# Twenty-two unread products on TensorE at the end of a two-layer diffusion trunk

## Chip, cores and metric

One core of a Trainium2 chip runs the whole kernel as one program. The metric is the device time of one execution in microseconds; lower is better.

## The reference

One inference step of a trunk with two layers, on 128 prompt tokens and 512 sample tokens with 1024 features each. Layer 0 is a Conformer convolution branch, layer 1 a bidirectional Mamba-2 (SSD) branch. The change touches the very end, the output projection of layer 1 and the RMSNorm after it:

```python
y = rms_norm(y.reshape(b, l, SSD_GROUPS, SSD_INNER // SSD_GROUPS), ...)
out = y @ w_out                       # 2048 -> 1024
yp = yp + gt_p * out_p                # gated residual, prompt
ys = ys + gt_s * out_s                # gated residual, sample
y_prompt = rms_norm(yp, final_norm_g) # x * rsqrt(mean(x*x) + 1e-6) * g
y_sample = rms_norm(ys, final_norm_g)
```

## The kernel before, in words

The activations lie transposed in on-chip memory: 8 tiles `x[0..7]` of 128 features by 640 tokens. The tokens are worked on in two halves of 320 (`HN`); half b holds columns `b * 320` to `b * 320 + 319`, 64 of the prompt and 256 of the sample. Every dense product is made in three terms from operands that are split into a high and a low part (`wh`, `wl` for weights, `yh`, `yl` for activations, type fp32r), 320 columns wide at the end of the program.

Layer 1 is written as many small generators (chains). A planner (`Order`) starts with estimated durations, picks the next operation over all chains by its estimated time and priority, and emits it; so the order of each engine's queue is fixed when the program is built. Each engine then works through its own queue strictly as it stands, and waits on counters of the other engines.

The end of the program, in the order that matters here:

- `last_products(b)`, first for half 1, then for half 0: for each of the 8 output tiles 4 steps of 3 products (line 1342, `o` in the rows), that is 12 products of 320 columns.
- `last_residual(b, m, ...)`: when tile m is done, VectorE adds it with its gate to `x[m]` (line 1311, two instructions), ScalarE squares it (line 1316, `sq`), GpSimd adds most squares into one accumulator (line 1321). The last tiles are scaled by the norm's weight on ScalarE at once (line 1325).
- `final(b)`: TensorE sums the squares over the features with a matmul against a column of ones (`column_sums`, line 177, one column each). It does so in two parts: the first two accumulators, then the last tile's square, `PARTS` of the tokens at a time. VectorE copies the first part (line 1357) and adds the second (line 1363) into `sm`; ScalarE takes the root (line 1364, `rc`); VectorE the reciprocal (line 1365); TensorE spreads it over all partitions (`spread`, line 182); VectorE multiplies the first tiles of `x` by it (line 1370); ScalarE copies it (line 1378, `rb`) and GpSimd multiplies the rest (line 1381); each finished tile is stored (line 1385, `o_y`), 160 KB at a time, 16 stores in all. `sm` and `rc` have one buffer each, which both halves use in turn.

In the program as built, the second part of half 1's sums, the first part of half 0's and the second part of half 0's stand on TensorE behind all the products, and both spreads stand behind these. An instruction of `column_sums` or `spread` on fp32 data shows as two matmul records in the trace, so 6, 12 and 6 sums and 6 and 6 spreads.

Of the kernel before, what the change touches and what calls it, by code (L numbers as in the profile page):

```python
# [7 lines left out]
F32 = mybir.dt.float32  # L8
# [5 lines left out]
P = 128  # L14
NT = 640
NP = 128
HN = 320
# [24 lines left out]
def trunk(ctx: ExitStack, tc: tile.TileContext, a: dict):  # L42
# [5 lines left out]
    V, S, G, T = nc.vector, nc.scalar, nc.gpsimd, nc.tensor  # L48
# [6 lines left out]
    def c(name, i=0, n=1):  # L55
        o = _C[name][0] + i
        if o >= NCST:
            return cst0[0][:, o - NCST : o - NCST + n]
        return cst[:, o : o + n]
# [36 lines left out]
    def gain(l, m, cd):  # L96
        return mod[l][:, 8 + m // 2, m % 2, cd : cd + 1]
# [75 lines left out]
    def column_sums(ps, tiles, parts=FIVE):  # L173

        for i, (t0, nt) in enumerate(parts):
            for n, t in enumerate(tiles):
                last = T.matmul(ps[0:nt, i : i + 1], lhsT=t[:, t0 : t0 + nt], rhs=ones[:, 0:1], start=n == 0, stop=n == len(tiles) - 1)
        return last

    def spread(ps, col, parts=FIVE):  # L180
        for i, (t0, nt) in enumerate(parts):
            last = T.matmul(ps[:, t0 : t0 + nt], lhsT=col[0:nt, i : i + 1].broadcast_to([nt, P]), rhs=eye[0:nt, 0:nt], start=True, stop=True)
        return ps[:, 0 : parts[-1][0] + parts[-1][1]], last
# [55 lines left out]
    def mm(name):  # L239
        return pp.tile([P, 2, 512], F32, tag="mm", bufs=2, name=name)  # L240
# [51 lines left out]
    with tc.tile_pool(name="l0", bufs=1) as lp:  # L292
# [33 lines left out]
        for i in range(3):  # L326
            t = lp.tile([P, 2, 30], F32, name=f"eb{i}")
# [191 lines left out]
        yh, yl, scaled = [], [], []  # L519
# [97 lines left out]
    if True:  # L617
# [8 lines left out]
        for i in range(2):  # L626
            t = lp.tile([P, 646], F32, name=f"up{i}")
# [19 lines left out]
        def tr(name):  # L647
            return lp.tile([P, NT], F32, tag="yhl", bufs=8, name=name)[:, 0:384]
# [4 lines left out]
        xr, rp, e, q, t, u, v, one = (tr(n) for n in ("xr", "rp", "e", "q", "t", "u", "v", "one"))  # L653
# [8 lines left out]
        PE, ACT, VE, PO, SP, VL = range(6)  # L662

        class Order:
# [12 lines left out]
            def post(self, key, t):  # L677
                assert key not in self.keys, key
                self.keys[key] = t

            def put(self, name, t):
                self.rings[name].append(t)

            def start(self, gen, ready=0.0, name=None):
                self.count += 1
                ch = [gen, ready, PRIO.get(name or gen.__name__, 1), self.count, None, None]
                self.chains.append(ch)
                self.advance(ch, None)
# [70 lines left out]
        post, put, start = run.post, run.put, run.start  # L759

        def op(eng, dur, fn, table=None):
            return "op", ((eng, dur, fn, table),)
# [4 lines left out]
        def key(*ks):  # L767
            return ("key",) + ks

        def get(name):  # L770
            return "get", name
# [8 lines left out]
        def vec(n):  # L780
            return 0.12 + 0.001 * n
# [107 lines left out]
        grp = [{} for _ in range(NG)]  # L889
# [387 lines left out]
        w3 = {}  # L1277
# [25 lines left out]
        accs = {0: [], 1: []}  # L1303
# [3 lines left out]
        def last_residual(b, m, ps, ring):  # L1307
            tok = slice(b * HN, b * HN + HN)
            for cd, sl in SEGS:
                xv = x[m][:, tok][:, sl]  # L1310
                t = yield op(VE, vec(sl.stop - sl.start) + 0.08, lambda: V.scalar_tensor_tensor(out=xv, in0=ps[:, sl], scalar=gain(1, m, cd), in1=xv, op0=ALU.mult, op1=ALU.add))
            put(ring, t)
            nm, bufs = SQ[b]
            yield get(nm)
            sq = lp.tile([P, 512], F32, tag=nm, bufs=bufs, name="sq")[:, 0:HN] if b == 0 else lp.tile([P, HN], F32, tag=nm, bufs=bufs, name="sq")
            t = yield op(ACT, 0.47, lambda: S.activation(out=sq, in_=x[m][:, tok], func=AF.Square))
            if m == 0 or m > KD - 3:
                accs[b].append(sq)
            else:
                yield key(("acc", b, m - 1))  # L1320
                t = yield op(PO, 0.85, lambda: G.tensor_add(out=accs[b][0], in0=accs[b][0], in1=sq))
                put(nm, t)
            post(("acc", b, m), t)
            if m >= KD - REST[b]:
                t = yield op(ACT, 0.56, lambda: S.activation(out=x[m][:, tok], in_=x[m][:, tok], func=AF.Copy, scale=c("fg", m)))
                post(("scaled", b, m), t)

        def last_products(b):
            yield key(("norm", 3, b), *[("products", 1)] * (b == 0))
            tok = slice(b * HN, b * HN + HN)  # L1330
            yh, yl = grp[3]["yh"], grp[3]["yl"]
            for mp in range(4):
                yield key(("w3", mp), ("res", 2 * mp, 2), ("res", 2 * mp + 1, 2))
                for j in range(2):
                    ring = "b" if j and b == 0 else "mm"
                    yield get(ring)
                    ps = mm("o2")[:, 0, 0:HN] if ring == "mm" else pq.tile([P, 512], F32, tag="b", bufs=3, name="o2")[:, 0:HN]
                    for k in range(4):
                        def step():
                            wh, wl = (z_[:, j * 128 : j * 128 + 128] for z_ in w3[k, mp])  # L1340
                            for n, (wt, t_) in enumerate(((wh, yh[k]), (wh, yl[k]), (wl, yh[k]))):
                                T.matmul(ps, lhsT=wt, rhs=t_[:, tok], start=k == 0 and n == 0, stop=k == 3 and n == 2)  # L1342
                        t = yield op(PE, 0.44, step)
                    start(last_residual(b, 2 * mp + j, ps, ring), t, f"residual{b}")
            post(("products", b), t)


        PARTS = ((0, 128), (128, 128), (192, 128))

        def final(b):  # L1350
            tok = slice(b * HN, b * HN + HN)
            yield key(("acc", b, KD - 3), ("acc", b, KD - 2))
            yield get("b")
            ps = pq.tile([P, 512], F32, tag="b", bufs=3, name="rps")
            yield op(PE, 0.84, lambda: column_sums(ps[:, 384:387], accs[b][:2], PARTS))
            sm, rc = (gp.tile([P, 3], F32, tag=nm, bufs=1, name=nm) for nm in ("sm", "rc"))
            yield op(VE, 0.16, lambda: V.tensor_copy(out=sm, in_=ps[:, 384:387]))

            yield key(("acc", b, KD - 1))
            t = yield op(PE, 0.6, lambda: column_sums(ps[:, 388:391], accs[b][2:], PARTS))  # L1360
            for _ in range(3):
                put(SQ[b][0], t)
            yield op(VE, 0.16, lambda: V.tensor_add(out=sm, in0=sm, in1=ps[:, 388:391]))
            yield op(ACT, 0.26, lambda: S.activation(out=rc, in_=sm, func=AF.Sqrt, scale=1.0 / 1024, bias=epsb), "sqrt")
            yield op(VE, 0.16, lambda: V.reciprocal(out=rc, in_=rc))
            cell = []
            yield op(PE, 0.8, lambda: cell.append(spread(ps, rc, PARTS)[0]))
            start(final_rest(b, cell, tok), run.clock[PE])
            for k in range(KD - REST[b]):
                t = yield op(VE, 0.54, lambda: V.scalar_tensor_tensor(out=x[k][:, tok], in0=x[k][:, tok], scalar=c("fg", k), in1=cell[0], op0=ALU.mult, op1=ALU.mult))  # L1370
                start(store(k, tok), t)
            put("b", t)

        def final_rest(b, cell, tok):

            yield get("yo")
            rb = lp.tile([P, 512], F32, tag="yo", bufs=2, name="rb")[:, 0:HN]
            yield op(ACT, 0.47, lambda: S.copy(out=rb, in_=cell[0]))
            yield key(*[("scaled", b, k) for k in range(KD - REST[b], KD)])
            for k in range(KD - REST[b], KD):  # L1380
                t = yield op(PO, 0.87, lambda: G.tensor_mul(out=x[k][:, tok], in0=x[k][:, tok], in1=rb))
                start(store(k, tok), t)

        def store(k, tok):
            yield either((SP, 0.5, lambda: nc.sync.dma_start(out=a["o_y"][:, k, tok], in_=x[k][:, tok])), (ACT, 0.5, lambda: nc.scalar.dma_start(out=a["o_y"][:, k, tok], in_=x[k][:, tok])), bias=0.2)
# [154 lines left out]
        with tc.manual_schedule():  # L1540
# [12 lines left out]
            pq = ctx.enter_context(tc.tile_pool(name="l1ps", bufs=1, space=PSUM))  # L1553
# [12 lines left out]
            for g in range(3):  # L1566
                start(free_bc(g), 0.0)
            start(last_products(1), 0.0, "products1")
            start(last_products(0), 0.0, "products0")
            start(final(1), 0.0, "final1")  # L1570
# [100 lines left out]
```

## Time and profile before

| | us |
|---|---|
| median of 3 runs | 1117.86 (1117.59 to 1118.91) |
| profiled execution, its time | 1117.72 |
| its span | 1115.9 |
| TensorE busy | 1067.5 (96%) |
| VectorE busy | 831.1 (74%) |
| ScalarE busy | 573.4 (51%) |
| GpSimd busy | 493.3 (44%) |

The span is what the trace covers; 1.8 us of the profiled execution's time lie outside it. Busy shares are means over very different stages. The granted clock of TensorE is given as a share of 2.4 GHz: 1.00 is 2.4 GHz, 0.50 is 1.2 GHz.

### The profile page before, as it was taken

The numbers are of one execution on the slowest core, as the hardware profiler recorded it, in microseconds if no ns is written. First come the engines' busy times: TensorE is split into PE (matmuls) and PEld (weight loads), VectorE is DVE, ScalarE is ACT, GpSimd is POOL, SyncE is SP. The second block draws the span as 40 slices with busy tenths as digits, with TensorE's granted clock in tenths as the row PEclk, the third lists the DMA queues.
The fourth block names the chain that finished last, engine by engine and source line by source line (L and its number), as shares of the span: only waits on it lengthen the run. The fifth ranks groups of instructions, "written<-read, shape, count | busy, mean of one in ns | idle before, by whom it ended". The sixth has DMA issues, their size and how long they took to land.

```text
span 1115.9 us, 19084 instructions
## 1 busy us (share of the span) xinstructions
PE 1067.5 (96%) x7560; PEld 971.8 (87%) x7560; DVE 831.1 (74%) x1182; ACT 573.4 (51%) x994; POOL 493.3 (44%) x421
## 2 busy tenths in 40 slices
PE   6999999998998999899999999999999999999996
PEld 3898889797898999899989897899899888978896
DVE  2579999989899859623368978998766695777673
ACT  6544456455645356421266666584536472644442
POOL 1255797788778726600000046414541544254213
PEclk9999999999999999999999999999999999999997
DMA  9434224323321211432412274334343514343102
GB/s 362 166 118 147 95 95 133 111 85 126 101 68 60 77 48 38 146 110 67 142 40 95 72 156 117 87 103 115 86 115 104 118 63 114 104 114 87 57 20 94
DMA packets 79049, 115.95 MB, mean 104 GB/s; under 512 B 26096, under 2 KB 49008, under 8 KB 78960
## 3 DMA queue, kind: packets, MB, share of 16 engines
q1 hardware_dynamic: 78240, 113.91, 34.4%
q8 instruction: 59, 0.97, 0.4%
q10 hardware_dynamic: 720, 0.82, 0.2%
q14 instruction: 30, 0.25, 0.1%
HBM read 109.80 MB, written 4.92 MB: 103 GB/s over the span
## 4 chain that ended last, share of the span: by engine, by line
PE 71%; DVE 14%; ACT 6%; issue 3%; DMA 3%; POOL 1%; SPq 1%; POOLq 0%; DVEq 0%; ACTq 0%
PE pz L833 8%; PE o L833 8%; PE xs L833 6%; DVE cva L361 3%; PE o L1342 3%; PE po L1114 2%; PE pst L1051 2%; PE B L833 2%; PE py L1182 2%; DVE xs L875 2%; DVE cn L524 2%; ACT wh L78 2%; PE C L833 1%; PE o__5398 L148 1%; PE o__4929 L148 1%
## 5 line engine op out<-in xcount | busy, mean ns | idle before, releaser
L361 DVE SCALAR_TENSOR_TENSOR cva<-v,cst,cva 128x550 f32<-128x550 f32 (+12 forms) x386 | 286.0, 815 | 10.2 <-ACT cva L354 8.7
L80 POOL TENSOR_TENSOR wl<-wf,wh 128x1024 fp32r<-128x1024 f32 (+1 forms) x50 | 119.1, 2382 | 122.2 <-ACT wh L78 117.4
L78 ACT CAST wh<-wf 128x1024 fp32r<-128x1024 f32 (+1 forms) x75 | 71.5, 956 | 180.0 <-PE o__4929 L148 37.4
L390 POOL TENSOR_TENSOR cv<-cv,tp 128x490 f32<-128x490 f32 (+3 forms) x94 | 113.4, 1211 | 14.1 <-ACT cv L388 9.4
L795 ACT CAST wh<-wf 128x1024 fp32r<-128x1024 f32 x53 | 55.5, 1047 | 82.1 <-PE o L833 27.8
L799 DVE TENSOR_TENSOR wl<-wf,wh 128x1024 fp32r<-128x1024 f32 x51 | 69.2, 1357 | 32.9 <-ACT wh L795 32.4
L833 PE MATMUL o<-yhl,wh 128*128 128x320 f32 x384 | 92.1, 327 | 0.0
L385 ACT ACTIVATE tp<-v,cst 128x490 f32<-128x490 f32 (+3 forms) x94 | 65.8, 716 | 40.6 <-POOL cv L390 40.5
L833 PE MATMUL pz<-h_hi,wh 128*128 128x384 f32 (+1 forms) x256 | 84.6, 330 | 0.5 <-ACT up L862 0.5
L1120 POOL TENSOR_TENSOR y<-y,yo 128x512 f32<-128x512 f32 x32 | 44.7, 1397 | 80.9 <-DVE yo L1118 80.8
L833 PE MATMUL pz<-h_hi,wl 128*128 128x384 f32 (+1 forms) x256 | 79.1, 309 | 0.0
L833 PE MATMUL pz<-h_lo,wh 128*128 128x384 f32 (+1 forms) x256 | 79.0, 309 | 0.0
L833 PE MATMUL xs<-h_hi,wh 128*128 128x384 f32 (+1 forms) x224 | 77.4, 346 | 0.0
L80 DVE TENSOR_TENSOR wl<-wf,wh 128x512 fp32r<-128x512 f32 (+1 forms) x25 | 27.2, 1087 | 66.3 <-ACT wh L78 66.2
L833 PEld LDWEIGHTS o<-yhl,wh 128*128 128x128 f32 x384 | 63.9, 188 | 7.8 <-issue 7.8
L875 DVE SCALAR_TENSOR_TENSOR xs<-up,cst,xs 128x642 f32<-128x642 f32 x64 | 69.0, 1079 | 2.2 <-ACT xs L873 0.8
L833 PE MATMUL xs<-h_hi,wl 128*128 128x384 f32 (+1 forms) x224 | 69.3, 309 | 0.0
L833 PE MATMUL xs<-h_lo,wh 128*128 128x384 f32 (+1 forms) x224 | 69.2, 309 | 0.0
L833 PE MATMUL o<-yhl,wl 128*128 128x320 f32 x192 | 59.2, 309 | 0.0
L989 POOL TENSOR_TENSOR gb<-gb,cols 128x512 f32<-128x512 f32 x20 | 24.9, 1246 | 75.8 <-DMA gb<-acd 75.8
L995 ACT ACTIVATE gf<-gf,cols 128x128 f32<-128x128 f32 x160 | 49.8, 392 | 16.6 <-DVE gf L991 16.5
L628 POOL MEMSET up<- 128x2 f32 x2 | 0.2, 100 | 117.2 <-DVE h_lo L219 117.2
(685 smaller groups left out, 3406.7 us busy)
## 6 DMA issues: line engine op xcount, KB each, us to landing
wf<-w_in SPq DMA_DIRECT2D x48, 512.0 KB, 3.6
wa<-w_ada SPq DMA_DIRECT2D x64, 256.0 KB, 4.8
wf<-w_out SPq DMA_DIRECT2D x24, 512.0 KB, 3.7
wf<-w_xbc SPq DMA_DIRECT2D x24, 512.0 KB, 3.7
gf<-acd SPq DMA_DIRECT2D x40, 256.0 KB, 4.8
wa<-w_ada SPq DMA_DIRECT2D x16, 512.0 KB, 10.2
wf<-w_z SPq DMA_DIRECT2D x16, 512.0 KB, 3.8
gb<-acd SPq DMA_DIRECT2D x40, 128.0 KB, 4.7
```

What stands on the lines that cost most here:

```text
L78: S.copy(out=wh[:, :n], in_=wf[:, :n])
L80: sub.tensor_sub(out=wl[:, :n], in0=wf[:, :n], in1=wh[:, :n].bitcast(F32))
L361: V.scalar_tensor_tensor(out=rows(acc)[:, :, lo:hi], in0=rows(v)[:, :, lo + d : hi + d], scalar=w_dw(i, tap), in1=rows(acc)[:, :, lo:hi], ...
L385: S.activation(out=tp[:, :, 0 : hi - lo], in_=rows(v)[:, :, lo + d : hi + d], func=AF.Copy, scale=w_dw(i, tap))
L390: G.tensor_add(out=rows(out)[:, :, lo:hi], in0=rows(out)[:, :, lo:hi], in1=tp[:, :, 0 : hi - lo])
L795: S.copy(out=cell["wh"], in_=cell["wf"])
L799: e_.tensor_sub(out=cell["wl"], in0=cell["wf"], in1=cell["wh"].bitcast(F32))
L833: T.matmul(ps[:, b, at_ : at_ + t1 - t0], lhsT=w_, rhs=t_[:, t0:t1], start=k == 0 and n == 0, stop=k == nk - 1 and n == 2)
L875: t = yield op(VL, 0.89, lambda: V.scalar_tensor_tensor(out=acc, in0=u[:, d : d + PW], scalar=c("w_c", j * 5 + d), in1=acc, op0=ALU.mult, ...
L995: t = yield op(ACT, 0.39, lambda: S.activation(out=gv[:, h_, :], in_=gv[:, h_, :], func=AF.Exp, bias=cols1[ch][:, o8 + h_ : o8 + h_ + 1]), ...
L1120: t = yield op(PO, 1.29, lambda: G.tensor_add(out=y, in0=y, in1=yo))
L1342: T.matmul(ps, lhsT=wt, rhs=t_[:, tok], start=k == 0 and n == 0, stop=k == 3 and n == 2)
```

## The change

A function `warm(n)` makes n products of 320 columns from operands that are already there (the first high weight block of the last group and its first high activation tile). They all go to one PSUM tile, which nothing reads. They are called at two places, for half 0 only: 12 when `last_products(0)` has made its last product, and 10 directly after the second part of half 0's sums.

```diff
                     start(last_residual(b, 2 * mp + j, ps, ring), t, f"residual{b}")
+            if b == 0:
+                warm(12)
             post(("products", b), t)
+        idle = []
+
+        def warm(n):
+            if not idle:
+                idle.append(pq.tile([P, 512], F32, tag="tr", bufs=1, name="warm"))
+            for _ in range(n):
+                T.matmul(idle[0][:, 0:HN], lhsT=w3[0, 0][0][:, 0:128], rhs=grp[3]["yh"][0][:, 0:HN], start=True, stop=True)
...
-            t = yield op(PE, 0.6, lambda: column_sums(ps[:, 388:391], accs[b][2:], PARTS))
+            def last_sums():
+                column_sums(ps[:, 388:391], accs[b][2:], PARTS)
+                if b == 0:
+                    warm(10)
+            t = yield op(PE, 0.6, last_sums)
```

The planner is told nothing of the added work (its durations are the same), so only TensorE's queue differs. Here is the end of that queue as the piece that differs, from the last products of half 0 on; `o` is the projection, `rps` the sums (line 177: three instructions of half 1, six and three of half 0) and the spread (line 182: three of half 1, three of half 0), `warm` the new products.

```order
 L1342 MATMUL o_11201<-yhl,wh_10970 128x320 x2
 L1342 MATMUL o_11201<-yhl,wl_10971 128x320
+L1356 MATMUL warm<-yhl,wh 128x320 x12
 L177 MATMUL rps<-ones,sq 128x1 x12
+L1356 MATMUL warm<-yhl,wh 128x320 x10
 L182 MATMUL rps<-cst,rc 128x128 x6
```

The twelve stand ahead of all the sums that are left, the ten between the last sums (of half 0) and the first spread (of half 1). Neither group waits for another engine.

VectorE's queue at the same place is the same in both programs but for line numbers. In the change's numbers, line 1378 adds the second part of the sums, 1368 copies the first part, 1380 is the reciprocal and 1385 the first final product; the first, third and fifth row belong to half 1, the others to half 0.

```order
L1378 TENSOR_TENSOR sm<-sm,rps 128x3 [waits DVE_49,PE_49]
L1368 COPY sm<-rps 128x3 [waits PE_49,Activation_49]
L1380 RECIPROCAL rc<-rc 128x3
L1378 TENSOR_TENSOR sm<-sm,rps 128x3 [waits DVE_49,PE_49]
L1385 SCALAR_TENSOR_TENSOR x_67<-x_67,cst,rps 128x320 [waits PE_49]
L1380 RECIPROCAL rc<-rc 128x3 [waits Activation_49]
```

Nothing moved here. Half 0's copy stands ahead of half 1's reciprocal and waits for TensorE's first part of half 0's sums.

## Rows read from the trace of the kernel before

**Rows 1.** The page: busy time by engine, and the granted clock in 40 slices.

```profile
PE 1067.5 (96%) x7560; PEld 971.8 (87%) x7560; DVE 831.1 (74%) x1182; ACT 573.4 (51%) x994; POOL 493.3 (44%) x421
...
PEclk9999999999999999999999999999999999999997
```

**Rows 2.** Chain that ended last, from 1100 us: start, us, engine and line.

```profile
1101.24 0.48 DVE x L1311
...
1101.81 0.48 ACT sq L1316
...
1102.31 0.56 ACT x L1325
1102.87 0.20 ACT rc L1364
...
1103.09 0.17 DVE sm L1357
...
1103.31 0.83 PE rps L177 x6
1104.13 0.98 PE rps L182 x6
...
1105.14 0.56 DVE x L1370
...
1106.23 2.49 POOL x L1381 x3
```

**Rows 3.** Timeline of TensorE's matmuls from 1098 us: start, us, instructions; idle before.

```profile
1098.05 0.31 PE L1342 MATMUL o<-yhl,wl 128*128 128x320 f32 x1
...
1100.68 0.31 PE L1342 MATMUL o<-yhl,wl 128*128 128x320 f32 x1
1100.84 2.06 PE L177 MATMUL rps<-ones,sq 128*128 128x1 f32 x18
1103.31 0.83 PE L177 MATMUL rps<-ones,sq 128*128 128x1 f32 x6 [0.41 <-DVE sm L1357]
1104.00 1.11 PE L182 MATMUL rps<-cst,rc 128*128 128x128 f32 x6
1105.83 1.65 PE L182 MATMUL rps<-cst,rc 128*128 128x128 f32 x6 [0.73 <-DVE rc L1365]
```

**Rows 4.** Timeline of VectorE and of ScalarE from 1100 us.

```profile
1104.17 0.16 DVE L1363 TENSOR_TENSOR sm<-sm,rps 128x3 f32<-128x3 f32 x1 [0.84 <-PE rps L177]
...
1105.14 0.30 ACT L1364 ACTIVATE rc<-sm,epsb 128x3 f32<-128x3 f32 x1 [2.09 <-PE rps L182]
```

**Rows 5.** Windows of 1 us: busy by engine, clock, DMA share, GB/s.

```profile
268.00:269.00 1.00, 0.38 (x1) 0.38 (x2) 1.00 (x3) 1.00 (x2) 0.84 (x3) 0.65 0.00 0
...
353.00:354.00 1.00, 1.00 (x7) 1.00 (x7) 0.96 (x2) 0.99 (x2) 1.00 (x3) 0.82 0.00 0
...
1104.00:1105.00 1.00, 1.00 (x8) 0.81 (x7) 0.16 (x1) 0.00 (x0) 0.00 (x0) 0.79 0.00 0
1105.00:1106.00 1.00, 0.27 (x2) 0.17 (x2) 0.63 (x2) 0.57 (x2) 0.00 (x0) 0.50 0.00 0
```

**Rows 6.** Timeline of TensorE's matmuls around two earlier falls of the clock.

```profile
265.78 0.31 PE L157 MATMUL u__2784<-h_hi,wl 128*128 128x320 f32 x1
...
349.45 0.31 PE L157 MATMUL u__3647<-h_hi,wl 128*128 128x320 f32 x1
352.58 0.41 PE L157 MATMUL u__3754<-h_hi,wh 128*128 128x320 f32 x1 [2.81 <-ACT sz L441]
...
354.01 0.47 PE L157 MATMUL u__3754<-h_hi,wl 128*128 128x320 f32 x1
...
356.68 0.47 PE L157 MATMUL u__3754<-h_hi,wh 128*128 128x320 f32 x1
```

**Rows 7.** Windows of 0.25 us at the stores; columns as in Rows 5.

```profile
1107.65:1107.90 0.25, 0.00 (x0) 0.00 (x0) 0.25 (x1) 0.00 (x0) 0.25 (x2) 0.50 1.02 348
...
1114.40:1114.65 0.25, 0.00 (x0) 0.00 (x0) 0.00 (x0) 0.00 (x0) 0.00 (x0) 0.50 0.58 210
```

## The prediction

> **What bounds the kernel now.** I read the page first: TensorE is busy for 96% of the span, at the full clock (2.4 GHz) in every slice but the last [rows 1]. So anything that stands in its queue early costs time; but the change adds work only behind the last product, and there the question is another: who is waited for in the last 15 us? That is the second view, the chain of waits [rows 2]. The reader should see that TensorE's column sums at 1100.84 are not on it. The chain goes from the last product over VectorE's residual (1101.24), ScalarE's square (1101.81), its scaling of the tile (1102.31), half 1's root (1102.87) and VectorE's copy for half 0 (1103.09) to TensorE's last sums (1103.31), half 1's spread (1104.13) and the first final product (1105.14). Third, the timeline of TensorE [rows 3]: the 18 sums end at 1100.84 + 2.06 = 1102.90, so TensorE has a little slack there, and idles only 0.41 us before the last sums and 0.73 us before half 0's spread. Fourth, the windows [rows 5]: the clock falls to 0.50 (1.2 GHz) inside 1104 to 1105; a mean of 0.79 is 0.42 us at the low level, so it fell at 1104.58, in the middle of half 1's spread. Fifth, the transfers [rows 7]: from 1107.65 on the 16 DMA engines are full, at about 350 GB/s, for 27 windows of 0.25 us, and run dry at about 1114.55. The end of the program is thus the moment at which the stores begin, plus a fixed time for their bytes.
>
> **The price of a product.** From 1098.05 to 1100.68 TensorE starts 18 products of the added form, a third of them with the weight block that the one before used; 2.63 / 18 = 0.146 us each at the full clock [rows 3]. At the low clock, 354.01 to 356.68 holds ten: 0.267 us each [rows 6].
>
> **The twelve.** They wait for nothing and go ahead of the 18 sums: 12 x 0.146 = 1.75 us. The sums then start at 1102.59, and their modelled end is 1104.65. Hidden is only what the copy had to spare: a TensorE result reaches VectorE 0.03 us after its end (1104.17 against 1103.31 + 0.83) [rows 3, 4], so the copy could have run at 1102.93 and ran at 1103.09 [rows 2]. Slack 0.16, delay 1.75 - 0.16 = **1.59 us**: copy at 1104.68, last sums at 1104.90. Half 1's root does not get in the way: its six sums end at 1102.59 + 0.83 = 1103.42, the addition (0.16) and root (0.30) [rows 4] end at about 1103.9, ahead of the copy. Its reciprocal stands behind the copy on VectorE, as before, and is in time.
>
> **The ten.** The last sums take 0.69 us to the next instruction (1103.31 to 1104.00) [rows 3], so the ten start at 1105.59. Behind them on TensorE stands half 1's spread, whose reciprocal is ready by then: nothing hides them. At the full clock they cost 10 x 0.146 = 1.46 us, at the low clock 10 x 0.267 = 2.67.
>
> **The spread.** From its start to the first final product half 1's spread took 1104.00 to 1105.14, 1.14 us, with the clock falling in it. At the low clock half 0's shows the price: 1.65 + 0.03 = 1.68 us [rows 3]. At the full clock no row has it; the six sums, which load weights of the same form and stream one column, ended after 0.83 us [rows 3], and 127 more columns at 2.4 GHz are 0.05: an estimate of 0.83 + 0.05 + 0.03 = 0.91. So this step gives back 0.23 or costs 0.54 more.
>
> **Behind it** everything follows the first final product. Half 0's root waits for half 1's spread (one buffer `rc`; ScalarE stood 2.09 us for it) [rows 4], and moves along. A faster half 0's spread is worth nothing, as its products queue behind half 1's and the transfers are full by then [rows 7]. So the whole delay reaches the end. The added instructions issue no DMA, and no other queue changes.
>
> **Does the clock stay up?** The ten and the spread depend on it. The fall at 1104.58 came 3.75 us after the last 320-column product (1100.68 + 0.146), although TensorE was never idle for longer than 0.41 us in between: sums of one column did not hold it [rows 3, 5]. Two earlier falls: after the product at 265.78 the clock fell at 268.30 (0.65 is 0.70 us low), 2.4 us behind it; after the one at 349.45 it fell at 353.64, 4.0 us behind it and a full microsecond after products had come back at 352.58 [rows 5, 6]. With the change, 320-column products end at 1102.59 and come back at 1105.59, 3.0 us later, with sums between. The same three delays would put the fall at 1104.97, 1106.34 or 1106.63, each ahead of or inside the ten. The nearest row is the one of the same stretch, so I take 3.75 us: a fall at 1106.34, five of the ten at 0.146 and five at 0.267, 0.73 + 1.34 = 2.07 us, and the spread at the low price.
>
> **Sum, the likeliest case:** 1.59 + 2.07 + 0.54 = 4.20 us. The profiled execution took 1117.72, so 1121.92; it lies 0.14 under the median of the runs, and I give **1121.9**.
>
> The Trainium skill, page "TensorE: Matmul & The Clock Gate", section "Why this matters for your kernels", asks to keep TensorE busy and without long idle gaps between bursts, so that it stays at the full clock. By that rule a TensorE that never rests keeps its clock, and the change would come out as rival A below. The trace does not bear it out in this form: the clock fell while TensorE was busy with one-column sums.
>
> **Rivals.**
> - *A, the clock stays up* through sums, ten and spread. For it: the idle gaps shrink, and the ten begin before two of the three delays above have run out. Against: all three delays end before 1107.05, when the ten would be over. Sum: 1.59 + 1.46 - 0.23 = 2.82 us, 1120.5. Still slower.
> - *B, the clock falls before the ten:* 1.59 + 2.67 + 0.54 = 4.80, 1122.5; if the last sums slow down too, by no more than what parts six records at the low clock from six at the full one (1.65 - 0.83 = 0.8), up to 1123.3. This is the upper end of the likeliest case, not a different mechanism, and I keep it inside that chance.
> - *C, not slower: the 22 products cost next to nothing,* because equal weights and an equal operand, with no sum to add to, let TensorE run them into each other. Place: its queue, at both groups. Delay at price p, with the clock held: 22p - 0.16 - 0.23. It would be under 0.2% (2.24 us, about what a measurement of this kernel can tell from no change) for p under 0.12, and free products would give 1117.72 - 0.23 = 1117.5. Against it: a third of the products priced above repeat the weight block of their forerunner, and the mean is 0.146 all the same, and the trace has as many weight loads as matmuls, 7560 each [rows 1, 3].
> - That the change does not do what it says is excluded by the built order: both groups stand in the queue. But the waits it names, 0.41 and 0.73 us, are shorter than the 3.2 us it puts there.
>
> **How the numbers follow.** Likeliest case with B 0.53, A 0.36, C 0.09, something that I don't see and that helps 0.02. Slower by over 0.2% is the first two, 0.89; within 0.2% is C, 0.09; faster 0.02, since even free products gain only 0.02%. The range goes from A with half a microsecond more slack than I counted, 1120.0, to B with a part of the slower sums, 1123.1; it leaves out C and little else.
>
> **What would show it.** Right: after the last `o` product a block of 12 at 0.146 us each; the copy at about 1104.7 and the last sums at about 1104.9; a block of ten directly behind; the first final product 2.8 to 4.8 us later than 1105.14, and the run-dry of the transfers later by the same. The windows then tell the likeliest case from A: 0.50 before 1107, or 1.00 until the spread is over. Wrong: a pitch of the added products far below 0.146; last sums that start before 1104; a first store that is late while the end is not.

## The result, and the profile after

The change made the kernel slower: 1121.38 us (median of 13 runs, 1118.70 to 1127.36) against 1117.94 (13 runs, 1114.75 to 1119.94), a ratio of 1.0030 with a 95% interval of 1.0018 to 1.0043, that is 3.4 us (2.0 to 4.8). The prediction was 1121.9, with a range of 1120.0 to 1123.1. The profiled execution took 1120.52 us, its span 1118.7.

TensorE's timeline of the change, the counterpart of [rows 3] (start, us, instructions; idle before):

```profile
1099.83 0.31 PE L1342 MATMUL o<-yhl,wl 128*128 128x320 f32 x1
1099.97 1.93 PE L1356 MATMUL warm<-yhl,wh 128*128 128x320 f32 x12
1101.73 2.06 PE L177 MATMUL rps<-ones,sq 128*128 128x1 f32 x18
1104.12 0.83 PE L177 MATMUL rps<-ones,sq 128*128 128x1 f32 x6 [0.32 <-DVE sm L1368]
1104.81 1.79 PE L1356 MATMUL warm<-yhl,wh 128*128 128x320 f32 x10
1106.40 1.48 PE L182 MATMUL rps<-cst,rc 128*128 128x128 f32 x6
1108.61 1.65 PE L182 MATMUL rps<-cst,rc 128*128 128x128 f32 x6 [0.72 <-DVE rc L1380]
```

The two traces don't reach this place at the same moment: the last `o` product starts at 1099.83 here and at 1100.68 before. So everything below is counted from that start. The last sums came 2.63 us behind it before (1103.31 - 1100.68), and come 4.29 us behind it now (1104.12 - 1099.83): the twelve delay them by **1.66 us**. The ten stand from 1104.81 to 1106.40: **1.59 us**. The spread takes from 1106.40 to the first final product at 1107.92, 1.52 us, where it took 1.14: **0.38 us**. Together 3.63 us, and so the first final product is 8.09 us behind the last `o` product, where it was 4.46 [rows 2, 3]. The time of the profiled execution is only 2.80 us above the one before (1120.52 - 1117.72), because the work ahead of this place was 0.85 us shorter: 3.63 - 0.85 = 2.78.

The two waits that the change fills are still there. The one ahead of the last sums went from 0.41 to 0.32 us, the one ahead of half 0's spread from 0.73 to 0.72. Both end with a result of VectorE, which works on what TensorE delivers: TensorE's sums came later, so VectorE's answer did too.

The chain of waits, the counterpart of [rows 2] (start, us, engine and line):

```profile
1102.90 0.91 PE rps L177 x8
...
1103.90 0.17 DVE sm L1368
...
1104.12 0.83 PE rps L177 x6
1104.95 1.65 PE warm L1356 x10
...
1107.92 0.56 DVE x L1385
```

Before, VectorE's copy into `sm` was reached over the residual, ScalarE's square and half 1's root; TensorE's 18 sums were not on that way. Now the way to the copy goes over these sums, and behind the last sums over the ten `warm` products: TensorE became the bound of this stretch.

The windows, the counterpart of [rows 5] and [rows 7] (columns as there):

```profile
1105.00:1106.00 1.00, 1.00 (x8) 1.00 (x8) 0.14 (x1) 0.00 (x0) 0.00 (x0) 1.00 0.08 16
1106.00:1107.00 1.00, 1.00 (x7) 1.00 (x6) 0.00 (x0) 0.00 (x0) 0.00 (x0) 0.64 0.00 0
...
1117.00:1117.25 0.25, 0.00 (x0) 0.00 (x0) 0.00 (x0) 0.00 (x0) 0.00 (x0) 0.50 0.93 358
1117.25:1117.50 0.25, 0.00 (x0) 0.00 (x0) 0.00 (x0) 0.00 (x0) 0.00 (x0) 0.50 0.33 113
```

The clock is at 1.00 up to 1106 and has a mean of 0.64 in the next window, which is 0.72 us at 0.50: it fell at 1106.28, near the end of the ten. The transfers run dry at about 1117.33 (a full quarter microsecond has a share of 1.02, so 0.33 of it is 0.08 us). That is 9.41 us behind the first final product. Before it was 1114.55 - 1105.14 = 9.41 as well: the whole delay reaches the end.

### The profile page after: what moved, and what is told of

Its sections match the earlier page's. It is cut to its first block, busy times and chain, and to the rows that moved or that the text cites. A ratio compares the mean times of both kernels' runs of the same rounds, so it can differ in the third digit from the quotient of the medians.

```text
span 1118.7 us, 19128 instructions
## 1 busy us (share of the span) xinstructions
PE 1069.0 (96%) x7582; PEld 975.1 (87%) x7582; DVE 828.8 (74%) x1182; ACT 573.6 (51%) x994; POOL 493.1 (44%) x421
## 4 chain that ended last, share of the span: by engine, by line
PE 71%; DVE 14%; ACT 5%; DMA 4%; issue 3%; POOL 1%; SPq 1%; POOLq 0%; DVEq 0%; ACTq 0%
PE pz L833 8%; PE o L833 8%; PE xs L833 6%; DVE cva L361 3%; PE o L1342 3%; PE po L1114 2%; PE pst L1051 2%; PE B L833 2%; PE py L1182 2%; DVE xs L875 2%; DVE cn L524 2%; ACT wh L78 2%; PE C L833 1%; PE o__5398 L148 1%; PE o__4929 L148 1%
```

## The experiments

**The theory:** TensorE works through its queue in order, so a product that nobody reads costs its full pitch (the time from its start to the next start) as soon as the wait that it can fill is used up; 3.2 us of products stand in 0.4 and 0.7 us of waits. **Rivals:** the products run into each other and cost little (rival C of the prediction); the delay comes from the clock rather than from the queue; the products do hold the clock and what loses time is their number or their place.

In the table, "sums", "first final" and "dry" are the starts of the last sums and of the first final product, and the moment at which the transfers run dry, each in us behind the start of the last `o` product. The fall of the clock is in us of the span. The last column is "dry" less "first final". In e4 and e8, where half 1 is finished ahead of half 0's products, the sums and the first final product are half 0's.

```
run            last o    sums   first final   clock falls at   dry     dry - first
before         1100.68   2.63   4.46          1104.58          13.87   9.41
the change     1099.83   4.29   8.09          1106.28          17.50   9.41
e1_twelve      1101.06   4.29   6.19          1106.57          15.6    9.4
e2_ten         1102.52   2.62   8.08          1105.35          17.5    9.4
e3_waits_only  1099.18   2.62   4.26          1107.88          13.67   9.41
e4_early_half  1100.99   1.88   4.44          1105.39          10.14   5.70
e5_again       1100.74   4.30   7.40          1110.84          16.8    9.4
e6_double      1101.63   6.05   10.35         1109.25          19.75   9.40
e7_ten_behind  1104.59   2.61   4.87          1108.01          14.27   9.40
e8_early_fill  1105.58   1.88   5.16          1108.76          10.87   5.71
```

**e1 and e2: each group alone.**

```diff
             def last_sums():
                 column_sums(ps[:, 388:391], accs[b][2:], PARTS)
-                if b == 0:
-                    warm(10)
```

```diff
-            if b == 0:
-                warm(12)
             post(("products", b), t)
```

> Only the twelve products behind the last projection product; the ten are left out. Measure: time from the start of the last 320-column product of the projection to the start of the last sums (six records) and to the first final product; 2.63 and 4.46 us before, 4.29 and 8.09 with the change. Queue theory (TensorE works in order, slack 0.16 us): last sums at 4.2 to 4.3, first final product at 5.8 to 6.7 by where the clock falls, time +1.3 to +2.2 us. Rival (the twelve fit into TensorE's wait and the ten make the whole loss): last sums at 2.6 to 2.8, first final product at 4.3 to 5.0, time the same.

> Only the ten products behind the last sums; the twelve are left out. Same measure. Queue theory: last sums unchanged at 2.6 to 2.7; first final product at 4.46 plus 1.46 to 2.67 for the ten, minus 0.23 to plus 0.54 for the spread: 5.7 to 7.7; time +1.2 to +3.2 us. Rival (half 1's spread waits for its root anyway, so the ten are hidden): first final product at 4.2 to 5.0, time the same.

The twelve alone: 1.0019 (1.0003 to 1.0035) times the kernel before, +2.1 us (0.3 to 3.9); in the trace the first final product is 1.73 us later. The ten alone: 1.0014 (0.9997 to 1.0031), +1.6 us (-0.3 to 3.5), which the timing alone can't tell from nothing. The trace of e2 shows why one number would not do for it. TensorE's timeline there:

```profile
1102.52 0.31 PE L1342 MATMUL o<-yhl,wl 128*128 128x320 f32 x1
...
1105.14 1.27 PE L177 MATMUL rps<-ones,sq 128*128 128x1 f32 x6 [0.41 <-DVE sm L1366]
1106.27 3.01 PE L1354 MATMUL warm<-yhl,wh 128*128 128x320 f32 x10
1109.08 1.48 PE L182 MATMUL rps<-cst,rc 128*128 128x128 f32 x6
```

In this execution the clock fell at 1105.35, within the last sums. They took 1.13 us to the next instruction instead of 0.69 (0.44 more), the ten took 2.81 (1.59 in the change), and the spread 1.52 (0.38 more than before): 0.44 + 2.81 + 0.38 = 3.63 us together, as measured from the last `o` product (8.08 - 4.46 = 3.62). The clock fell ahead of the ten, as in case B of the prediction, and in this execution less than half of the added products made the first final product as late as all 22 did in the one shown above; it is later than the 5.7 to 7.7 us expected, because the sums slowed down too. So the ten cost between 1.55 us (e5, below) and 2.81, by when the clock falls. The two timed differences add up to 3.7 us against 3.4 for the whole change.

**e3: no more products than the waits hold.** Two behind the first part of half 0's sums, four behind half 1's spread, and none elsewhere.

```diff
-            yield op(PE, 0.84, lambda: column_sums(ps[:, 384:387], accs[b][:2], PARTS))
+            def first_sums():
+                column_sums(ps[:, 384:387], accs[b][:2], PARTS)
+                if b == 0:
+                    warm(2)
+            yield op(PE, 0.84, first_sums)
...
-            yield op(PE, 0.8, lambda: cell.append(spread(ps, rc, PARTS)[0]))
+            def spread_out():
+                cell.append(spread(ps, rc, PARTS)[0])
+                if b == 1:
+                    warm(4)
+            yield op(PE, 0.8, spread_out)
```

> Products only where TensorE was idle: two behind the first part of half 0's sums (idle 0.41 us), four behind half 1's spread (idle 0.73 us), none elsewhere. Theory (the waits are real but short): last sums at 2.6 to 2.8, first final product at 4.2 to 5.0, time the same within 0.2%. Rival 1 (each product costs its price wherever it stands): last sums at 2.9, first final product at 4.8 or later, half 0's spread 0.6 later, time +0.3 to +0.9. Rival 2 (six products hold the clock and the end follows the clock): half 0's spread in 0.9 to 1.1 us where it took 1.65, time -0.5 or more. If the clock stays up and the time does not move, the stores are the bound and not the clock.

Measured: 0.9991 (0.9974 to 1.0008), not to be told from no change. TensorE's timeline of e3:

```profile
1099.33 2.06 PE L177 MATMUL rps<-ones,sq 128*128 128x1 f32 x18
1101.25 0.54 PE L1354 MATMUL warm<-yhl,wh 128*128 128x320 f32 x2
1101.80 0.83 PE L177 MATMUL rps<-ones,sq 128*128 128x1 f32 x6
1102.49 0.91 PE L182 MATMUL rps<-cst,rc 128*128 128x128 f32 x6
1103.16 0.83 PE L1354 MATMUL warm<-yhl,wh 128*128 128x320 f32 x4
1104.13 0.93 PE L182 MATMUL rps<-cst,rc 128*128 128x128 f32 x6
```

The windows of e3 where the transfers run dry (columns as in [rows 5]):

```profile
1112.50:1112.75 0.25, 0.00 (x0) 0.00 (x0) 0.00 (x0) 0.00 (x0) 0.00 (x0) 0.50 0.93 358
1112.75:1113.00 0.25, 0.00 (x0) 0.00 (x0) 0.00 (x0) 0.00 (x0) 0.00 (x0) 0.50 0.39 138
```

The last sums start 2.62 us behind the last `o` product, as before: the added products are hidden. The clock stayed up through both spreads. Half 1's takes 0.95 us to the first final product (1.14 before) and half 0's 0.93 instead of 1.65. All that this gives at the end is the 0.2 us of half 1's: the transfers run dry 9.41 us behind the first final product, as in every trace of this order, though half 0's spread was 0.7 us shorter. So what the filled waits can win here is 0.2 us, which a measurement of this kernel doesn't see.

**e5 to e7: the change again, more products, and the ten in a place where nobody waits.** e5 is the change unaltered, for a second trace. e6 and e7:

```diff
-                warm(12)
+                warm(24)
```

```diff
             def last_sums():
                 column_sums(ps[:, 388:391], accs[b][2:], PARTS)
-                if b == 0:
-                    warm(10)
...
+            def spread_out():
+                cell.append(spread(ps, rc, PARTS)[0])
+                if b == 1:
+                    warm(10)
+            yield op(PE, 0.8, spread_out)
```

(e7 has no twelve either.)

> The changed kernel once more, for another moment of the clock's fall. Queue theory: last sums again 4.2 to 4.4 us behind the start of the last 320-column product of the projection, whatever the clock does (up to 0.5 more if it falls before them); first final product between 7.2 (clock at 1.00 through the first spread) and 9.5 us (at 0.50 from the last sums on), 8.09 in the run shown. If the clock alone made the loss, a run with the clock at 1.00 would have 4.3.

> 24 products in place of the twelve, ten as in the change. Queue theory: 12 more at 0.146 us, all on the path: last sums at 6.0 to 6.1 us behind the last product, first final product 1.75 later than with 12, 9.0 to 11.0, time +4.5 to +6.5 us. Rival (products without an accumulation run into each other, so the count hardly matters): last sums at 4.3 to 4.8.

> Only the ten, and behind half 1's spread in place of ahead of it. Theory (the end is the first store plus the bytes; half 0's chain has slack): first final product at 4.2 to 5.0 as before, half 0's spread 0.7 to 2.0 us later than before against half 1's, the transfers still run dry 13.5 to 14.5 us after the last product, time the same within 0.2%. Rival (ten products cost 1.5 to 2.7 us wherever they stand): transfers run dry 15.3 us after the last product or later.

e5 and e6 had one run each, 1120.71 and 1124.56 us, beside 1118.40 for before (median of 19 runs). TensorE's timeline of e5:

```profile
1105.73 1.71 PE L1356 MATMUL warm<-yhl,wh 128*128 128x320 f32 x10
1107.28 0.83 PE L182 MATMUL rps<-cst,rc 128*128 128x128 f32 x6
```

The window of e5 in which the clock fell (columns as in [rows 5]):

```profile
1110.00:1111.00 1.00, 0.00 (x0) 0.00 (x0) 1.00 (x3) 0.00 (x0) 1.00 (x3) 0.92 0.42 142
```

TensorE's timeline of e6:

```profile
1101.77 3.69 PE L1356 MATMUL warm<-yhl,wh 128*128 128x320 f32 x24
1105.30 2.06 PE L177 MATMUL rps<-ones,sq 128*128 128x1 f32 x18
...
1108.37 2.29 PE L1356 MATMUL warm<-yhl,wh 128*128 128x320 f32 x10
1110.46 1.48 PE L182 MATMUL rps<-cst,rc 128*128 128x128 f32 x6
```

The same view of e7:

```profile
1107.89 1.53 PE L182 MATMUL rps<-cst,rc 128*128 128x128 f32 x6
1109.08 2.77 PE L1354 MATMUL warm<-yhl,wh 128*128 128x320 f32 x10
1111.68 0.83 PE L182 MATMUL rps<-cst,rc 128*128 128x128 f32 x6
```

In e5 the clock stayed at 1.00 until 1110.84, beyond both spreads: this is rival A, seen. The ten took 1.55 us and the spread to the first final product (1108.14) 0.86, so all in all 7.40 - 4.46 = 2.94 us. The change makes the end later with the clock up, too. In e6 24 products take 3.53 us, 0.147 each, and the sums come 1.76 us later than with twelve (6.05 - 4.29): the price goes on unchanged, and rival C, products that run into each other, is out. The first final product of e6 is 5.89 us later than before, with 3.42 of it in the sums, 2.09 in the ten (some four of them behind the fall at 1109.25) and the rest in the spread.

e7 has the ten at the low clock, 2.60 us of them, in front of half 0's spread, and is not slower: 0.9996 (0.9980 to 1.0012). Half 0's spread starts 2.22 us behind the first final product, where it was 0.69 (1105.83 - 1105.14) [rows 2, 3], and the transfers still run dry 9.40 us behind it. The first final product itself is 4.87 us behind the last `o` product instead of 4.46, because the clock fell 0.12 us into half 1's spread, not in its middle. Near the end of the ten, at about 1111.42, the clock came back to 1.00, and half 0's spread took 0.83 us instead of 1.65; that moved the end no more than its later start did. So products cost by their number only where what stands behind them is waited for.

**e4 and e8: what bounds the end instead.** If the end is the begin of the stores plus their bytes, half of the bytes can leave earlier. In e4 the planner ranks half 1's `final` ahead of half 0's products, by one number of its table; no product is added. e8 is e4 with two products behind the first part of half 0's sums and five behind the second, to hold the clock for half 0's spread.

```diff
-"final1": 3
+"final1": -5
```

```diff
+                if b == 0:
+                    warm(2)
+            yield op(PE, 0.84, first_sums)
...
+                if b == 0:
+                    warm(5)
             t = yield op(PE, 0.6, last_sums)
```

> No unread products. The planner's priority of half 1's final chain goes from last to first, so that its last sums and its spread stand between half 0's products and its 8 stores leave while TensorE still works. Theory (the end is the start of the stores plus their bytes at 350 GB/s): half 1's 12 records cost TensorE 1.3 to 1.5 us ahead of the last product, but behind it only 8 stores are left (3.7 us where 16 took 7.0 to 7.5); the transfers run dry 9.5 to 11 us after the start of the last product where it was 13.9; time -2 to -3.5 us, 1114.5 to 1116. Rival (the end is set by half 0's chain on VectorE and GpSimd, which half 1's final products now hold up): transfers run dry 12.5 to 14 us after the last product, time the same or up to 1.5 us longer.

> The kernel with half 1's final chain first, plus two unread products behind the first part of half 0's sums and five behind the second, where TensorE idled 0.34 and 0.79 us in that kernel's run. Theory: they fit into the waits; half 0's first final product stays at 4.3 to 4.6 us behind the last product (4.44 without them) and the time within 0.2% of that kernel, at best 0.3 us less in runs where the clock would have fallen before the spread. Rival (even there they hold up what stands behind them): first final product at 5.0 or later, time +0.5 to +1.0 us over that kernel.

e4: 0.9974 (0.9958 to 0.9990), 2.9 us faster than before (1.1 to 4.7). TensorE's timeline of e4 at half 0's spread:

```profile
1104.46 0.93 PE L182 MATMUL rps<-cst,rc 128*128 128x128 f32 x6 [0.79 <-DVE rc L1365]
```

VectorE's timeline of e4 at the first final product:

```profile
1105.43 0.55 DVE L1370 SCALAR_TENSOR_TENSOR x<-x,cst,rps 128x320 f32<-128x320 f32 x1 [1.03 <-PE rps L182]
```

The window of e4 where the transfers run dry (columns as in [rows 5]):

```profile
1111.00:1111.25 0.25, 0.00 (x0) 0.00 (x0) 0.00 (x0) 0.00 (x0) 0.00 (x0) 0.50 0.54 190
```

Only half 0's 8 stores are left behind the first final product, and the transfers run dry 5.70 us behind it instead of 9.41. The difference of 3.71 us is the time of the other 8 stores: 8 x 160 KB in 3.71 us are 353 GB/s, the rate of the full windows. So the end does follow the bytes.

e8 doesn't improve on it: 0.9986 (0.9970 to 1.0002). TensorE's timeline of e8:

```profile
1108.12 1.14 PE L1354 MATMUL warm<-yhl,wh 128*128 128x320 f32 x5
1109.06 1.64 PE L182 MATMUL rps<-cst,rc 128*128 128x128 f32 x6
```

In e8 the clock fell at 1108.76 in spite of the products, in the middle of the five; the spread took 1.64 us at the low clock, and the first final product was 0.72 us later than in e4 (5.16 against 4.44), as the rival expected, but not for its reason. The spread starts 3.48 us behind the last `o` product, and 3.47 in e4: the added products held up nothing, and the 0.72 us are the clock's. That the filled waits hold the clock is thus not to be relied on: it held in the one trace of e3 and not in that of e8.

**e9 to e11: the same idea upstream.** In layer 0 the clock falls twice behind waits of TensorE [rows 5, 6]. There the added products can be fitted to the waits: ten of 192 columns behind tile 12's product of the input projection and 14 behind tile 36's, into columns of the same PSUM tile that nobody reads. e10 is e9 with e4's number. e11 is the control: the same instructions with 2 columns each.

```diff
             dense_all(ps, wh, wl, h, [k * 128 for k in range(KD)])
+            for _ in range({12: 10, 36: 14}.get(mt, 0)):
+                T.matmul(ps[:, 1, HN:512], lhsT=wh[:, 0:128], rhs=h[0][0][:, 0:192], start=True, stop=True)
```

(In e11 `HN : HN + 2` and `0:2`.)

> No unread products at the end. Instead 10 and 14 unread products of 192 columns in layer 0, directly behind the projection tiles 12 and 36, ahead of the places near 266 and 350 us where TensorE stood 2.2 and 2.8 us and the clock then fell to 0.50 for 3.4 us in most of the runs seen. They go to spare columns of the tile just made. The planner of layer 0 also moves some VectorE and TensorE instructions by a few places. Theory (unread products pay where a wait is longer than they are and much full-width work follows): the granted clock stays at 1.00 around 266 to 275 and 350 to 360, the start of the last projection product comes earlier by up to 1.7 us for each fall avoided, time -1.5 to -3.5 us. Rival (they delay the reader of the tile they write to, or the moved instructions cost as much): the clock stays up, but the time is the same or longer.

> The same products in layer 0 together with half 1's final chain first. Theory: both gains add, since they lie in different stages: time -4 to -6.5 us against before, 1112 to 1114.5. Rival: layer 0's part gains nothing, and the time is that of half 1's chain alone, -2 to -3.5 us.

> The control for the products in layer 0: the same 10 and 14 at the same two places, but of 2 columns in place of 192. VectorE's order in layer 0 is that of the run with 192 columns but for four rows, so it shares the planner's moves, and TensorE is given as many instructions. Theory (the gain is the clock, and the clock is held by columns, not by instructions): the clock falls again at one or both of the places near 266 and 350 us in most executions, and the time lies 1.5 to 3.5 us above the 1113.75 of the run with 192 columns, ratio to before 0.997 to 1.000. Rival (the gain came from the planner's moves): ratio to before 0.995 to 0.9965, with or without falls.

e9: 0.9961 (0.9948 to 0.9974), 4.4 us faster than before. e10: 0.9957 (0.9941 to 0.9972), so the gains of e4 and e9 did not add up; why is open. e11: 0.9959 (0.9944 to 0.9974), 4.6 us faster, in the range of its rival. The windows of before around both places (columns as in [rows 5]):

```profile
265.00:275.00 10.00, 7.81 (x45) 7.72 (x45) 10.00 (x17) 5.38 (x11) 9.38 (x12) 0.83 0.15 43
345.00:362.00 17.00, 14.19 (x87) 13.92 (x86) 16.89 (x25) 8.19 (x11) 15.07 (x17) 0.90 0.20 62
```

The same windows of e9:

```profile
265.00:275.00 10.00, 8.90 (x65) 8.82 (x65) 10.00 (x17) 5.94 (x10) 9.38 (x11) 1.00 0.09 23
345.00:362.00 17.00, 17.00 (x121) 17.00 (x120) 15.08 (x22) 8.88 (x12) 15.94 (x21) 1.00 0.25 78
```

And of e11, the control:

```profile
265.00:275.00 10.00, 8.92 (x46) 8.84 (x45) 10.00 (x17) 5.52 (x11) 9.37 (x12) 0.66 0.06 10
345.00:362.00 17.00, 17.00 (x121) 17.00 (x120) 15.16 (x22) 9.95 (x14) 16.14 (x18) 1.00 0.19 63
```

e9 alone looked like a proof: the clock at 1.00 in both stretches (0.83 and 0.90 before), and 4.4 us gained. The control takes that reading away. In e11 the clock fell in the first stretch, to a mean of 0.66, lower than before, and the gain is the same within the intervals. And e3, which adds nothing in layer 0, kept 1.00 through both waits as well. TensorE's timeline of e9:

```profile
265.12 1.25 PE L322 MATMUL u__2784<-h_hi,wh 128*128 128x192 f32 x10
...
347.41 1.70 PE L322 MATMUL u__3657<-h_hi,wh 128*128 128x192 f32 x14
348.94 0.34 PE L157 MATMUL u__3778<-h_hi,wh 128*128 128x320 f32 x1
```

The same view of e11:

```profile
265.80 1.17 PE L322 MATMUL u__2784<-h_hi,wh 128*128 128x2 f32 x10
...
268.50 0.64 PE L157 MATMUL u__2855<-h_hi,wh 128*128 128x320 f32 x1 [1.08 <-DVE ssum L404]
...
350.80 1.62 PE L322 MATMUL u__3657<-h_hi,wh 128*128 128x2 f32 x14
352.28 0.39 PE L157 MATMUL u__3778<-h_hi,wh 128*128 128x320 f32 x1
```

In both, the next tile's products follow the 14 directly: the wait of 2.81 us on ScalarE's `sz` that stood here before [rows 6] isn't filled, it is gone, whatever the width: the `sz` that the next tile waits for ends at 347.3 in e9 and at 350.7 in e11, ahead of the 14. The 14 themselves take 1.53 us in e9 (347.41 to 348.94) and 1.48 in e11 (350.80 to 352.28), so this place is about 1.3 us shorter than before. The extra instructions also changed the order in which layer 0's other work is put on the engines (about a tenth of its VectorE instructions stand elsewhere in both programs).

What the clock has to do with the gain is read from all runs and not from one trace each. The runs of before differ in their mean granted clock, from 0.985 (1122.88 us) to 0.994 (1114.72) beside e9, and 0.001 of it goes with 0.73 us (20 runs; 0.79 over the 17 beside e11). The mean over the runs is 0.9928 in e9 against 0.9900 before, and 0.9929 in e11 against 0.9892. By these rates an estimated 2.0 of e9's 4.4 us and 2.9 of e11's 4.6 go along with a higher clock, and the rest does not. So the narrow products come with as high a clock as the wide ones, and with the same gain within the intervals (the medians are 0.6 us apart, on different chips): the width, which was to hold the clock, is not seen to pay. What both programs share, and before lacks, is the order and the added instructions. Whether the vanished wait is why the mean clock is higher is not shown; which of the moved instructions brings the rest stays open too.

## Why the prediction was right, point by point

- **What bounds the end**, the begin of the stores and then their bytes: right. 9.4 us from the first final product in each trace of this order, and 3.71 less with half of the stores (e4). "A faster half 0's spread is worth nothing": right (e3), and a later one costs nothing either (e7).
- **The twelve**, 1.75 less a slack of 0.16: the block measured 1.76, and the delay 1.66 instead of 1.59. The slack was taken from a reaction of VectorE of 0.03 us [rows 3, 4]; at this copy it was 0.09 (1103.81 to 1103.90 in the chain).
- **The ten**, 1.46 to 2.67, likeliest 2.07: ends measured at 1.55 (e5) and 2.81 (e2), so the bounds hold to within 0.14; the shown execution has 1.59. The likeliest value was over-sized by 0.48. The clock fell at almost the time that I gave (1106.28 against 1106.34), but that was luck, and the ten were by then nearly over: the whole stretch began 0.85 us earlier on the span's time axis, and the fall came 4.55 us behind the end of the last 320-column product ahead of the sums (1101.73), not 3.75. A delay that had been read once was carried over as if fixed.
- **The spread**, +0.54 or -0.23: measured 0.38 (1.52 us at the low clock, not 1.68) and -0.28 (0.86 in e5; the estimate was 0.91). Right in sign; the cost was over-sized by 0.16.
- **The sum**: 3.63 us in the shown execution against 4.20, 2.94 in e5 against rival A's 2.82; the timed difference of 3.4 lies between. The likeliest case and rival A are thus not two outcomes of which one holds: the clock fell within the 22 products' stretch in one execution and behind it in the other. The mechanism, a queue whose work is waited for, was right; that the median came within 0.5 us of 1121.9 says less, as the interval of the difference alone goes from 2.0 to 4.8 us and the sum was 0.57 us too high for the execution shown.
- **Rival C** is refuted by e6, and the rule of the Trainium skill (page "TensorE: Matmul & The Clock Gate", section "Why this matters for your kernels") that a busy TensorE keeps its clock came true in e5 and e3. It did not in the change's own shown execution, nor in e1, e2, e6, e7 or e8, where the clock fell although TensorE had idled no longer than 0.41 us since the last `o` product. Where it came true with all 22 products, it gave back 0.28 us of the 3.2 that they cost.

## What to carry to other kernels

Work that fills a wait is free only up to the wait's length, and only if the wait's end doesn't hang on the engine that is filled: 22 products of 0.146 us were put where 0.4 and 0.7 us were free, and both waits stayed. Ask what stands behind the added work and who waits for that; the ten cost 1.6 to 2.8 us ahead of half 1's spread and nothing behind it. And when filler makes a kernel faster, run it once with filler that can't do what it is there for: in e11 that took the explanation away, not the gain. Where the runs of one program differ by more than the effect, look at the mean clock of all runs, and put no gain down to the clock of one trace.

## What the runs showed of the hardware that was not expected

**The same queue gets another clock from one execution to the next.** Layer 0 is the same program in before and in e3. TensorE's timeline of before at one of its waits there:

```profile
268.62 0.64 PE L157 MATMUL u__2845<-h_hi,wh 128*128 128x320 f32 x1 [2.19 <-DVE ssum L402]
```

The window behind it (columns as in [rows 5]):

```profile
269.00:270.00 1.00, 1.00 (x5) 1.00 (x5) 1.00 (x3) 0.93 (x2) 1.00 (x2) 0.50 0.07 16
```

TensorE's timeline of e3 at the same wait:

```profile
269.28 0.42 PE L157 MATMUL u__2845<-h_hi,wh 128*128 128x320 f32 x1 [2.20 <-DVE ssum L402]
```

And a window behind it:

```profile
271.00:272.00 1.00, 1.00 (x9) 1.00 (x8) 1.00 (x2) 1.00 (x4) 1.00 (x1) 1.00 0.00 0
```

TensorE idles equally long in both, and comes back to a clock of 0.50 in one and 1.00 in the other. The traces differ in how many such falls they have upstream, and at the extremes with them in when the last `o` product starts: 1099.18 in e3 with one, 1102.52 in e2 and 1104.59 in e7 with four. It is not falls alone: e1 with two starts it at 1101.06, before with three at 1100.68. e4 and e8 share one order up to there, and start it at 1100.99 (one fall) and 1105.58 (three, two of them longer). This goes along with the spread of the runs of before, 1114.2 to 1123.0 us, which is larger than the effect of the change; only because the parts were read from an anchor inside each trace, the last `o` product, can a single execution be compared at all.

**The clock fell at short pauses, and with TensorE busy.** The Trainium skill, page "TensorE: Matmul & The Clock Gate", section "Why this matters for your kernels", warns of long idle gaps between bursts. Here the clock fell a microsecond behind a pause of 2.81 us [rows 6] and within one of 2.19 us (the row at 268.62 above, and [rows 5]); at the end of before it fell in the middle of half 1's spread, behind 24 one-column sums and no pause longer than 0.41 us [rows 3, 5]; and in e8 it fell among the added 320-column products, with no idle time since the last `o` product. In e11 ten products of 2 columns took 1.17 us, hardly less than the ten of 192 columns in e9 with their 1.25. The clock fell in e11 at 267.76, in the pause behind them, and not in e9; with one trace of each, and e3 holding 1.00 there with no added product at all, that is not shown to be due to the width.
